# A two-layer hybrid block on one core: triangular inverse and retention issued earlier, six feed-forward columns for one half with their down products under the norm

## The chip, the cores and the metric

One core of a Trainium2 chip runs the whole program. The metric is the device time in microseconds (us), the median of several runs. The engines are TensorE (PE, with its weight loads shown as PEld), VectorE (DVE), ScalarE (ACT), GpSimd (POOL) and SyncE (SP), whose queue issues nearly all transfers. Each engine works through its own instructions in program order; they wait for each other through semaphores.

## What is computed

Two layers over x of 1024 tokens by 1024 columns, float32, each with a mixer of four parts and a feed-forward part:

```python
def hybrid_layer(x, ...):
    p = rms_norm(x, g_pre_mix) @ w_in            # 1024 -> 2824 columns
    y_a = pool_mixer(a_pool, ...)                # windowed means
    y_b = retention_mixer(r_q, r_k, r_v, r_g, cos, sin)   # chunks of 128, 4 heads
    y_c = spatial_gating_mixer(s_u, s_v, ...)
    y_d = deltanet_mixer(d_qkv, d_z, d_b, d_a, ...)       # chunks of 64: triangular solve, then a scan
    x = x + rms_norm(concat(y_a, y_b, y_c, y_d) @ w_out, g_post_mix)
    h = rms_norm(x, g_pre_ffn)
    a, b = split(h @ w_up)                       # 2 x 2816 columns
    a = causal_dwconv(a, conv_w) + conv_b
    return x + rms_norm((gelu(a) * b) @ w_down, g_post_ffn)
```

## The kernel before

The tokens are taken in two halves of 512 (`HALF`), each as four blocks of 128 (`NB`). Every large matrix product is made of three products: weights and activations are split in a high part, cast by ACT (`whi`, L202; L207 for activations), and a low part, the rest, by DVE (`wlo`, L203; L208). `unit()` loads, casts and splits one piece of weights.

For layer l and half h, `win(l, h)` computes the input products and the four mixers, and `out(l, h)` the output product and both norms. In the second layer the feed-forward part is done differently from the first: up products by a scheme of sums and differences of token rows (`build` makes seven combinations A11, S1, S2, A12, S3, Q4, A22; `up_f` makes for one column block f of 128 columns the products of both halves, or of the second half only), with gated results in a DRAM array `gD`, and then a down phase over all 22 blocks f, whose sums stand in eight tiles `acc`. For the first few f, the first half's up product is instead made in the plain way (`plain_up`, L1029 on), before `build`: eight of them, five ahead of `out(1, 1)` and three behind it. These are the work that covers the two norms.

What sets the order: the program is written as a sequence of steps, and a scheduler places every instruction in its engine's queue by its own estimate of the times, with the order of the code as priority; `high_priority(offset)` moves instructions forward. In `win` a string gives the order of ten steps: for `win(1, 1)` it is `ORD1`, with z, s, p, n for input units, g and q for two mixers, u for the retention's units, r for the retention and b for `dn_back`. Ahead of them stands `dn_front`, which makes the triangular matrices `LT`, `AT` and sends their diagonal 32x32 blocks through DRAM to the tile `A`, 64 blocks on 64 partitions. `dn_back` then has three parts: 31 steps on DVE that invert the diagonal blocks in place,

```python
for i in range(1, 32):
    V.scalar_tensor_tensor(pr[:, 0:i, 0:i], A[:, 0:i, 0:i], -1.0, ...)      # L833
    V.tensor_reduce(A[:, 0:i, i], pr[:, 0:i, 0:i], AX.X, ALU.add)           # L835
```

two passes of the inverse through DRAM (d2 to `XT`, and d3 to the small tiles x, which `dn_solve` loads), and four `dn_solve` and four `dn_scan`, one for each block of 128 tokens, whose instructions take turns. `dn_solve` is the chain L876, L884, L893, L899, L908/L910 on PE with DVE and ACT between; `dn_scan` (L938, L953, L956) ends with a head norm on ACT and DVE and a transpose on PE (L962), whose result times `zf` is the last quarter of y. `out(1, 1)` needs all of y.

The last stage, `end_block`, multiplies each block's sum by the norm's weights (`gx`, L1213), half of it on POOL and half on DVE, and adds x.

Of the kernel before, what the change touches and what calls it, by code (L numbers as in the profile page):

```python
# [19 lines left out]
P = 128  # L20
# [15 lines left out]
ORD1 = "zspgqunbr"  # L36
# [21 lines left out]
NPRE, NHALF = 5, 8  # L58
# [60 lines left out]
class Net:  # L119
# [30 lines left out]
    def down_phase(self):  # L150
        self.phase(("pa", 8), ("pr", 2), ("py", 2), ("pw", 6), ("pg", 6))
# [268 lines left out]
    def win(self, l, h, hT, pre=None):  # L420
# [107 lines left out]

        def do_back():
            self.dn_back(l, qf, R["zf"], sc, dn, FAST and (l, h) in QUICK)  # L530
# [4 lines left out]
        steps = dict(n=do_rg, f=do_first, z=do_z, s=do_su, p=do_pool, g=do_sgu, q=do_pmix, u=do_runits, r=do_ret, b=do_back)  # L535
# [287 lines left out]
    def dn_back(self, l, qf, zf, sc, dn, fast):  # L823
        nc, pp, tmp, st, pm = self.nc, self.pp, self.tmp, self.state[l], self.pm[l]
        V = nc.vector
        LT, AT, R0, kt, A2, Dv = (dn[k] for k in ("LT", "AT", "R0", "kt", "A", "Dv"))
# [20 lines left out]
        X = dict(d3=d3, LT=LT, AT=AT, R0=R0, kt=kt, Dv=Dv, XT=XT, qf=qf, zf=zf, sc=sc, MC={})  # L847
# [190 lines left out]


# [6 lines left out]
    def rows(self, l):  # L1046
        names = ("A22", "A12", "Q4", "S3", "S2", "S1", "A11")
        self.A = {}
        for n in names[::-1]:
# [42 lines left out]
    def up_f(self, l, f, halves):  # L1092
# [18 lines left out]
        with self.tc.high_priority(offset=2000):  # L1111
# [52 lines left out]
    def down_full(self, l):  # L1164
# [4 lines left out]
        groups = [[0, 1]] + [list(range(f, f + 4)) for f in range(2, NF, 4)]  # L1169
        for fs in groups:  # L1170
            us, gs = [], []
            for f in fs:
                us.append(self.unit(t["wD"][l, f]))
                r = self.r4("graw")
                nc.sync.dma_start(r, self.gD[l][f])
                g = self.pg.tile([P, 2, SEQ], F32R, tag="g", name="g")
                with self.tc.high_priority(offset=2000):
                    self.split(g[:, 0], g[:, 1], r)
                gs.append(g)
            last = fs is groups[-1]  # L1180
            for b in range(2 * NB):
                tb = slice(b * P, b * P + P)
                for n in range(2):
                    s = slice(n * 512, n * 512 + 512)
                    ps = self.ps() if n else self.pq()
                    for i in range(len(fs)):
                        g, u = gs[i], us[i]
                        nc.tensor.matmul(ps, g[:, 0, tb], u[0][:, s], start=i == 0, stop=False)
                        nc.tensor.matmul(ps, g[:, 0, tb], u[1][:, s], start=False, stop=False)
                        nc.tensor.matmul(ps, g[:, 1, tb], u[0][:, s], start=False, stop=i == len(fs) - 1)  # L1190
# [9 lines left out]
    def end_block(self, l, b, acc, gpost):  # L1200
# [3 lines left out]
        xb = self.py.tile([P, D], F32, tag="xb", name="xb", bufs=6)  # L1204
# [4 lines left out]
        g = self.py.tile([P, D], F32, tag="gx", name="gx")  # L1209
        for n in range(2):  # L1210
            s = slice(n * 512, n * 512 + 512)
            nc.scalar.activation(sq[:, s], acc[:, s], AF.Square, accum_out=ss[:, n:n + 1])
            (nc.gpsimd if n == 0 else V).tensor_tensor(g[:, s], acc[:, s], gpost[:, s], ALU.mult)  # L1213
# [84 lines left out]
    def run(self):  # L1298
# [6 lines left out]
        for l in range(DEPTH - 1):  # L1305
# [8 lines left out]
            y = self.win(l + 1, 1, hT)  # L1314
# [8 lines left out]
        for f in range(2):  # L1323
            self.up_f(l, f, (1,))
        self.build(l, 0)
        half = list(range(2, NHALF))
        for f in range(NHALF, NF):
# [83 lines left out]
```

## Time and profile before

| | us |
|---|---|
| median of 3 runs | 2557.73 (2556.59 to 2560.81) |
| profiled execution | 2557.02, span 2555.2 |
| PE busy | 2431.4 (95% of the span) |
| DVE busy | 1773.3 (69%) |
| ACT busy | 968.4 (38%) |
| POOL busy | 267.0 (10%) |
| mean granted PE clock | 0.974 of full |

The span is what the profile shows; 1.8 us of the profiled execution lie around it. Stages of interest, by their place in the span: `win(1, 1)` from about 1500 to 1800 us, with the bare solve and scan from 1660 to 1728; `out(1, 1)` to about 1853; three plain f to 1888; `build` from 1896 to about 1945; the up phase to 2283; the down phase from 2296 to 2544; the end to 2555. In rows with a bracket, the bracket gives the engine's idle time before the row and what ended it. The granted clock is given as a share of full speed.

### The profile page before, as it was taken

The page shows a single profiled execution, that of the slowest core. Times are in us where ns is not written, and L with a number is a line of the kernel's source. Part 1 is how long each engine was busy: PE and PEld are TensorE (multiplying, and loading weights), DVE is VectorE, ACT ScalarE, POOL GpSimd, SP SyncE. Part 2 cuts the span into 40 slices and gives each one's busy share as a digit, 9 for nine tenths or more (in the row PEclk, how much of TensorE's full clock was granted, in tenths as well). Part 3 has the DMA queues.
Part 4 walks back from the last instruction along what each step waited for, and adds up shares of the span by engine and source line. Part 5 has one row for each costly group of instructions (what it writes and reads, how often), then busy time and mean ns, then how long its engine had stood idle before and what let it go on. Part 6 is the DMA issues. An engine that isn't in the chain of part 4 may idle for free. (4 is left out here: it accounts for less than half of the span.)

```text
span 2555.2 us, 36529 instructions
## 1 busy us (share of the span) xinstructions
PE 2431.4 (95%) x14116; PEld 2031.3 (79%) x14116; DVE 1773.3 (69%) x3657; ACT 968.4 (38%) x1509; POOL 267.0 (10%) x359
## 2 busy tenths in 40 slices
PE   8989998999999999999999999959978999979998
PEld 7968987877788987787788897847967888868886
DVE  8895799765655898855665688956577776653537
ACT  6333452423332553332332355212445444432212
POOL 2221113000000013100000003220011000000001
PEclk9999998999999999999999999968989999999999
DMA  5233442322223552322223354212553222233312
GB/s 182 76 90 102 137 148 72 97 76 83 84 86 124 166 166 69 99 80 79 75 91 97 128 181 165 81 35 72 169 189 112 91 100 87 83 119 128 132 66 83
DMA packets 98482, 274.54 MB, mean 107 GB/s; under 512 B 30258, under 2 KB 30578, under 8 KB 97796
## 3 DMA queue, kind: packets, MB, share of 16 engines
q1 hardware_dynamic: 94532, 259.55, 31.3%
q0 software_dynamic: 3776, 12.65, 1.5%
q8 instruction: 111, 1.82, 0.3%
q14 instruction: 63, 0.52, 0.1%
HBM read 234.39 MB, written 37.78 MB: 107 GB/s over the span
## 5 line engine op out<-in xcount | busy, mean ns | idle before, releaser
L202 ACT CAST whi<-raw 128x1024 fp32r<-128x1024 f32 (+1 forms) x298 | 310.6, 1049 | 679.8 <-PE psg L213 205.4
L212 PE MATMUL psg<-hT,whi 128*128 128x512 f32 x1280 | 510.6, 399 | 2.9 <-ACT whi L202 1.3
L213 PE MATMUL psg<-hT,whi 128*128 128x512 f32 x1280 | 509.0, 398 | 0.2 <-DVE hT L371 0.2
L214 PE MATMUL psg<-hT,wlo 128*128 128x512 f32 x1280 | 508.8, 399 | 0.0
L203 DVE TENSOR_TENSOR wlo<-raw,whi 128x1024 fp32r<-128x1024 f32 (+1 forms) x275 | 338.8, 1237 | 169.5 <-ACT whi L202 165.1
L212 PEld LDWEIGHTS psg<-hT,whi 128*128 128x128 f32 x1280 | 242.1, 189 | 57.5 <-ACT whi L202 1.9
L213 PEld LDWEIGHTS psg<-hT,whi 128*128 128x128 f32 x1280 | 241.8, 189 | 56.0 <-issue 0.6
L214 PEld LDWEIGHTS psg<-hT,wlo 128*128 128x128 f32 x1280 | 241.8, 189 | 55.8 <-issue 0.2
L1245 DVE TENSOR_TENSOR acc<-acc,psg 128x512 f32<-128x512 f32 x160 | 109.0, 686 | 74.7 <-PE psg L1240 74.1
L234 PE MATMUL psg<-wlo,hT 128*128 128x256 f32 (+1 forms) x512 | 148.5, 291 | 5.7 <-DVE wlo L203 5.7
L233 PE MATMUL psg<-whi,hT 128*128 128x256 f32 (+1 forms) x512 | 145.8, 288 | 2.2 <-DVE rqk L512 1.9
L235 PE MATMUL psg<-whi,hT 128*128 128x256 f32 (+1 forms) x512 | 147.3, 289 | 0.0
L233 PE MATMUL psg<-whi,y 128*128 128x256 f32 x512 | 142.5, 283 | 2.4 <-ACT raw L1007 0.9
L1104 ACT CAST w<-wraw 128x512 fp32r<-128x512 f32 x154 | 92.1, 620 | 137.5 <-PE psg L1090 67.4
L234 PE MATMUL psg<-wlo,y 128*128 128x256 f32 x512 | 143.2, 282 | 0.0
L235 PE MATMUL psg<-whi,y 128*128 128x256 f32 x512 | 142.9, 282 | 0.0
L1238 PE MATMUL psg<-whi,g 128*128 128x512 f32 x352 | 141.5, 404 | 0.0
L1105 DVE TENSOR_TENSOR w<-wraw,w 128x512 fp32r<-128x512 f32 x154 | 104.6, 698 | 49.9 <-ACT w L1104 49.4
L1239 PE MATMUL psg<-wlo,g 128*128 128x512 f32 x352 | 138.8, 394 | 0.0
L1240 PE MATMUL psg<-whi,g 128*128 128x512 f32 x352 | 138.6, 394 | 0.0
L833 DVE SCALAR_TENSOR_TENSOR pr<-A 64x1 f32<-64x1 f32 (+30 forms) x124 | 113.2, 913 | 5.8 <-POOL A L829 3.5
L234 PEld LDWEIGHTS psg<-wlo,hT 128*128 128x128 f32 x512 | 98.1, 192 | 8.9 <-DVE wlo L203 6.7
(471 smaller groups left out, 5092.4 us busy)
## 6 DMA issues: line engine op xcount, KB each, us to landing
raw<-in_wU SPq DMA_DIRECT2D x104, 512.0 KB, 3.5
raw<-in_wD SPq DMA_DIRECT2D x66, 512.0 KB, 3.8
raw<-in_wA SPq DMA_DIRECT2D x56, 512.0 KB, 3.6
wraw<-in_wU SPq DMA_DIRECT2D x22, 1024.0 KB, 4.9
raw<-in_wO SPq DMA_DIRECT2D x40, 512.0 KB, 3.8
raw<-in_wB SPq DMA_DIRECT2D x24, 512.0 KB, 3.6
xs<-xb SPq DMA_DIRECT2D x24, 512.0 KB, 3.8
graw<-gD SPq DMA_DIRECT2D x22, 512.0 KB, 4.8
```

What stands on the lines that cost most here:

```text
L202: nc.scalar.copy(hi[:, :n], raw[:, :n])
L203: eng.tensor_tensor(lo[:, :n], raw[:, :n], hi[:, :n].bitcast(F32), ALU.subtract)
L212: nc.tensor.matmul(ps, a[0], b[0], start=first, stop=False)
L213: nc.tensor.matmul(ps, a[0], b[1], start=False, stop=False)
L214: nc.tensor.matmul(ps, a[1], b[0], start=False, stop=last)
L233: self.nc.tensor.matmul(ps[:, :width], h0, hi[:, s], start=k == 0, stop=False)
L234: self.nc.tensor.matmul(ps[:, :width], h0, lo[:, s], start=False, stop=False)
L235: self.nc.tensor.matmul(ps[:, :width], h1, hi[:, s], start=False, stop=k == len(hT) - 1)
L833: V.scalar_tensor_tensor(pr[:, 0:i, 0:i], A[:, 0:i, 0:i], -1.0, A[:, 0:i, i].unsqueeze(1).to_broadcast([64, i, i]), ALU.mult, ALU.mult)
L1238: nc.tensor.matmul(ps, hi[:, tb], us[i][0][:, s], start=i == 0, stop=False)
L1239: nc.tensor.matmul(ps, hi[:, tb], us[i][1][:, s], start=False, stop=False)
L1240: nc.tensor.matmul(ps, lo[:, tb], us[i][0][:, s], start=False, stop=i == len(g0) - 1)
```

## The change

1. The 31 steps and what follows up to the small tiles x become a function of their own, `dn_inverse`, and step i. `ORD1` becomes "iunrzspgqxb": the inverse is first, then the retention with its units, then the rest, x and b.
2. Step x is new: the transposed activations of the first half (`to_hT`) and plain f 0 and 1 (`NFILL`). Four more (2 to 5) stand between `win(1, 1)` and `out(1, 1)`.
3. Six plain f instead of eight (`NPRE` = 6). So `up_f` runs for the second half alone for f 0 to 5, and for both for f 6 to 21. The calls for f 0 and 1 lose their priority of 2000.
4. Behind `out(1, 1)`, in place of three plain f, the new `plain_down`: down products of f 0 to 5 for the first half, 144 products of 512 columns, whose sums go to DRAM (`accD`).
5. The down phase loads `accD` into `acc[0]` to `acc[3]` and makes f 0 to 5 for the second half only, in groups of two and four. The split weights now lie in one tile with the split g (`g`, 4 x SEQ, six buffers); raw weights have two buffers (a pool `pw` of 2), raw g two.
6. `rows` allocates the seven combinations in the order of their use. `end_block` does both halves of gx on DVE; xb has 8 buffers, gx 4.

```diff
-ORD1 = "zspgqunbr"
+ORD1 = "iunrzspgqxb"
-NPRE, NHALF = 5, 8
+NPRE, NFILL = 6, 2
...
-        self.phase(("pa", 8), ("pr", 2), ("py", 2), ("pw", 6), ("pg", 6))
+        self.phase(("pa", 8), ("py", 2), ("pw", 2), ("pr", 2), ("pg", 6))
...
+        def do_inverse():
+            self.dn_inverse(dn)
+
         def do_back():
+            if "XT" not in dn:
+                self.dn_inverse(dn)
             self.dn_back(l, qf, R["zf"], sc, dn, FAST and (l, h) in QUICK)
...
+    def plain_down(self, l):
+        nc, V = self.nc, self.nc.vector
+        self.accD = self.pd.tile([HALF, D], F32, name="accD")
+        us, gs = [], []
+        for f in range(NPRE):
+            raw = self.pw.tile([P, WS], F32, tag="raw", name="raw", bufs=2)
+            nc.sync.dma_start(raw[:, :D], self.t["wD"][l, f])
+            if f < 3:
+                hi = self.pw.tile([P, WS], F32R, tag="hi", name="whi")[:, :D]
+                lo = self.pw.tile([P, WS], F32R, tag="lo", name="wlo")[:, :D]
+            else:
+                w = self.pp.tile([P, 2, D], F32R, tag="big", name="wbig", bufs=4)
+                hi, lo = w[:, 0], w[:, 1]
+            self.split(hi, lo, raw[:, :D])
...
+        for b in range(NB):
...
+                nc.scalar.copy(acc[:, s], ps)
+            nc.sync.dma_start(self.accD[tb], acc)
...
         acc = [self.pa.tile([P, D], F32, tag="acc", name=f"acc{b}") for b in range(2 * NB)]
-        groups = [[0, 1]] + [list(range(f, f + 4)) for f in range(2, NF, 4)]
+        for b in range(NB):
+            nc.sync.dma_start(acc[b], self.accD[b * P:b * P + P])
+        groups = [list(range(0, 2)), list(range(2, NPRE))] + [list(range(f, f + 4)) for f in range(NPRE, NF, 4)]
...
-            for b in range(2 * NB):
+            for b in range(NB if fs[0] < NPRE else 0, 2 * NB):
...
-            (nc.gpsimd if n == 0 else V).tensor_tensor(g[:, s], acc[:, s], gpost[:, s], ALU.mult)
+            V.tensor_tensor(g[:, s], acc[:, s], gpost[:, s], ALU.mult)
...
-        hT = self.to_hT(acc, True)
-        self.plain_up(l, 0, range(NPRE), hT)
+        self.plain_up(l, 0, range(NFILL, NPRE), keep["hT"])
         self.out(l, 1, y, True)
-        self.plain_up(l, 0, range(NPRE, NHALF), hT)
+        self.plain_down(l)
```

How the queues change at three places (a row: line, operation, output from inputs, shape, times in a row; some lines of `dn_solve` and `dn_scan` are 9 further on in the changed kernel, those of the retention 6).

PE before, in `win(1, 1)`, at the first solve: L367 are transposes of the next half's activations, L876 reads the small tiles x (x_99, x_100).

```order
L214 MATMUL psg<-hT_13388,wlo 128x512
L367 MATMUL psg<-ident,acc_13475 128x128
L367 MATMUL psg<-ident,acc_13476 128x128 x4
L367 MATMUL psg<-ident,acc_13477 128x128 x4
L876 MATMUL psm<-x_99,LT 32x32 x8
L876 MATMUL psm<-x_100,LT 32x32 x8
L884 MATMUL psm<-XT,x_99 32x32 x8
L884 MATMUL psm<-XT,x_100 32x32 x8
L893 MATMUL psm<-R_14590,XT 128x128 x8
L899 MATMUL psm<-AT,R_14590 64x128 x4
```

PE now, at the same place (L885 is the former L876):

```order
L586 MATMUL psm<-tmp,pm_7910 128x512
L885 MATMUL psm<-x_99,LT 32x32 x8
L885 MATMUL psm<-x_100,LT 32x32 x8
L214 MATMUL psg<-hT_15706,wlo 128x512
L212 MATMUL psg<-hT_15706,whi 128x512
L213 MATMUL psg<-hT_15708,whi 128x512
L214 MATMUL psg<-hT_15706,wlo 128x512
```

Between the steps of the solve there now stand 23, 20, 21, 6, 7, 3, 9, 2, 9, 19, 13 and 4 products of 512 columns of plain f 2 to 5 (136), and the retention's products are all ahead of it. Behind them come 36 products of `out` and the last two blocks of the scan without anything between, then 18 more of `out`, the last transpose (now L971) and the other 330.

DVE before, within the 31 steps (L203 is the low part of weights):

```order
L833 SCALAR_TENSOR_TENSOR pr<-A 64x27x27
L203 TENSOR_TENSOR wlo<-raw,whi 128x1024
L835 TENSOR_REDUCE A<-pr 64x27
L833 SCALAR_TENSOR_TENSOR pr<-A 64x28x28
L835 TENSOR_REDUCE A<-pr 64x28
L203 TENSOR_TENSOR wlo<-raw,whi 128x1024
```

DVE now, at the same steps: L280 to L286 are single links of the reciprocal root in the retention's head norm, and L625 applies it; the transpose L688 on PE waits for L625's `tmp`.

```order
L682 SCALAR_TENSOR_TENSOR ret_7938<-ret_7938,ck 128x128 x2
L841 TENSOR_REDUCE A<-pr 64x27
L285 SCALAR_TENSOR_TENSOR rt<-rt 128x4
L839 SCALAR_TENSOR_TENSOR pr<-A 64x28x28
L286 SCALAR_TENSOR_TENSOR rs<-rt,rs 128x4
L841 TENSOR_REDUCE A<-pr 64x28
L625 TENSOR_TENSOR tmp<-psm,rs 128x256
L618 TENSOR_REDUCE hs<-tmp 128x4
L839 SCALAR_TENSOR_TENSOR pr<-A 64x29x29
```

The head norm of the retention's first block of tokens is spread over steps 23 to 28, one link to a step or so, and that of the second block over steps 28 to 31 and the rows behind them.

SP before, from the up phase to the down phase (gD is the last up result, graw the loads of it, raw the weights):

```order
L1175 DMA graw<-gD_109 128x1024 x2
L1162 DMA gD_109<-c 128x1024
L1175 DMA graw<-gD_109 128x1024 x2
L200 DMA raw<-in_wD 128x1024 x2
L1175 DMA graw<-gD_109 128x1024 x2
```

SP now:

```order
L1211 DMA acc_20791<-accD 128x1024
L1219 DMA graw<-gD_109 128x1024 x2
L1203 DMA gD_109<-c 128x1024
L1219 DMA graw<-gD_109 128x1024
L1217 DMA wraw<-in_wD 128x1024 x3
```

One load of g instead of two stands ahead of the first weights, and four loads of `accD` ahead of both.

More of the change, by code (lines that the diff above doesn't have):

```diff
@@ L533, in do_first @@
             self.hT1 = self.first_norm(1)
[L535 removed]
+        steps = dict(n=do_rg, f=do_first, z=do_z, s=do_su, p=do_pool, g=do_sgu, q=do_pmix, u=do_runits, r=do_ret, b=do_back,
+                     i=do_inverse, x=mid)
         for k in (ORD0 if (l, h) == (0, 0) else ORD1 if (l, h) in QUICK else ORD):
@@ L821, in dn_front, with dn_inverse @@
         return dict(LT=LT, AT=AT, R0=R0, kt=kt, A=A, Dv=Dv)
-    def dn_back(self, l, qf, zf, sc, dn, fast):
-        nc, pp, tmp, st, pm = self.nc, self.pp, self.tmp, self.state[l], self.pm[l]
+    def dn_inverse(self, dn):
+        nc, pp = self.nc, self.pp
         V = nc.vector
-        LT, AT, R0, kt, A2, Dv = (dn[k] for k in ("LT", "AT", "R0", "kt", "A", "Dv"))
+        A2 = dn["A"]
         A = A2[0:64]
@@ L1037, in plain_up @@
             self.nc.sync.dma_start(self.gD[l][f, :, h * HALF:h * HALF + HALF], c)
+    def plain_down(self, l):
[12 more added lines that the diff above has]
+            self.split(hi, lo, raw[:, :D])
+            us.append((hi, lo))
+            r = self.pa.tile([P, HALF], F32, tag="acc", name="graw")
+            nc.sync.dma_start(r, self.gD[l][f, :, 0:HALF])
+            g = self.r4("g", F32R)
+            self.split(g[:, :HALF], g[:, HALF:], r)
+            gs.append((g[:, :HALF], g[:, HALF:]))
+        for b in range(NB):
+            tb = slice(b * P, b * P + P)
+            acc = self.pa.tile([P, D], F32, tag="acc", name="acc")
+            for n in range(2):
+                s = slice(n * 512, n * 512 + 512)
+                ps = self.ps()
+                for i in range(NPRE):
+                    nc.tensor.matmul(ps, gs[i][0][:, tb], us[i][0][:, s], start=i == 0, stop=False)
+                    nc.tensor.matmul(ps, gs[i][0][:, tb], us[i][1][:, s], start=False, stop=False)
+                    nc.tensor.matmul(ps, gs[i][1][:, tb], us[i][0][:, s], start=False, stop=i == NPRE - 1)
+                nc.scalar.copy(acc[:, s], ps)
+            nc.sync.dma_start(self.accD[tb], acc)
     def cbuf(self, name):
@@ L1046, in rows @@
     def rows(self, l):
-        names = ("A22", "A12", "Q4", "S3", "S2", "S1", "A11")
         self.A = {}
-        for n in names[::-1]:
+        for n in ("A11", "S1", "S2", "A12", "S3", "Q4", "A22"):
             hi = self.pA.tile([P, 4, 512], F32R, tag=f"{n}h", name=f"{n}h")
@@ L1090, in product, with up_f @@
             nc.tensor.matmul(ps, b[:, 1, s], ah[:, k, cs], start=False, stop=k == 3, skip_group_check=sk)
-    def up_f(self, l, f, halves):
+    def up_f(self, l, f, halves, ahead=2000):
         nc, pf = self.nc, self.pf[l]
@@ L1109, in add @@
             V.tensor_tensor(raw[:, o], raw[:, o], raw[:, a], ALU.add)
-        with self.tc.high_priority(offset=2000):
+        with self.tc.high_priority(offset=ahead):
             w11 = cast(2)
@@ L1313, in run, with fill @@
             acc = self.out(l + 1, 0, y)
-            y = self.win(l + 1, 1, hT)
+            keep = {}
+            def fill(a=acc):
+                keep["hT"] = self.to_hT(a, True)
+                self.plain_up(l + 1, 0, range(NFILL), keep["hT"])
+            y = self.win(l + 1, 1, hT, mid=fill)
         l = DEPTH - 1
-        hT = self.to_hT(acc, True)
-        self.plain_up(l, 0, range(NPRE), hT)
+        self.plain_up(l, 0, range(NFILL, NPRE), keep["hT"])
         self.out(l, 1, y, True)
-        self.plain_up(l, 0, range(NPRE, NHALF), hT)
+        self.plain_down(l)
         self.up_phase()
@@ L1322, in run @@
         self.build(l, 1)
-        for f in range(2):
-            self.up_f(l, f, (1,))
+        self.up_f(l, 0, (1,), 0)
+        self.up_f(l, 1, (1,), 0)
         self.build(l, 0)
-        half = list(range(2, NHALF))
-        for f in range(NHALF, NF):
+        half = list(range(2, NPRE))
+        for f in range(NPRE, NF):
             if half:
```

27 lines of the change are left out of this document (16 added, 11 removed).

## The prediction

> **What bounds it now.** First the page: PE is busy nearly all the time, so a gain is either work taken off PE or time in which PE waits or runs slowly.
>
> ```profile
> span 2555.2 us, 36529 instructions
> PE 2431.4 (95%) x14116; PEld 2031.3 (79%) x14116; DVE 1773.3 (69%) x3657; ACT 968.4 (38%) x1509; POOL 267.0 (10%) x359
> ```
>
> Second, the view of busy time by stretches, cut in the second layer where PE waits; the columns are stretch, its length, busy time of PE, PEld, DVE, ACT and POOL, clock, share of the DMA engines, GB/s.
>
> ```profile
> 1600.00:1660.00 60.00, 55.46 (x407) 49.99 (x406) 55.47 (x89) 14.95 (x19) 11.29 (x8) 1.00 0.28 81
> 1660.00:1676.00 16.00, 1.14 (x22) 0.80 (x21) 7.67 (x6) 2.04 (x2) 1.80 (x1) 0.61 0.47 112
> 1676.00:1692.00 16.00, 15.51 (x296) 13.61 (x296) 8.90 (x28) 6.13 (x20) 2.60 (x10) 0.86 0.03 6
> 1692.00:1708.00 16.00, 10.80 (x111) 7.65 (x108) 8.64 (x34) 1.95 (x6) 4.17 (x13) 0.78 0.11 35
> 1708.00:1728.00 20.00, 10.68 (x56) 8.31 (x56) 14.29 (x40) 5.75 (x12) 7.00 (x10) 0.50 0.02 7
> 1728.00:1742.00 14.00, 11.64 (x36) 8.48 (x37) 8.58 (x14) 1.96 (x4) 1.98 (x3) 0.50 0.10 39
> 1760.00:1888.00 128.00, 126.04 (x758) 110.03 (x756) 80.99 (x178) 53.86 (x86) 0.00 (x0) 1.00 0.49 165
> 1888.00:1945.00 57.00, 37.73 (x262) 34.60 (x260) 45.24 (x73) 28.57 (x53) 15.65 (x14) 0.79 0.45 155
> 2340.00:2380.00 40.00, 40.00 (x174) 32.36 (x173) 19.06 (x23) 8.11 (x8) 0.00 (x0) 1.00 0.29 100
> ```
>
> Length less busy time is idle; busy time times (1 - clock) is lost to the clock. From 1600 to 1742 that is 4.5 + 14.9 + 0.5 + 5.2 + 9.3 + 2.4 = 36.8 us idle and 0.4 + 2.2 + 2.4 + 5.3 + 5.8 = 16.1 us by the clock: 52.9 us, the largest sum the change can touch. Third, the waits of PE from 1655 to 1745, and the rows that end them.
>
> ```profile
> PE psm L876 <- DMA x<-d: 14.7, 1, 14.7
> PE psh L962 <- DVE tmp L619: 12.4, 3, 5.5
> 1675.20 1.42 PE L876 MATMUL psm<-x,LT 128*32 128x32 f32 x32 [14.72 <-DMA x<-d]
> 1701.39 0.69 PE L962 MATMUL psh<-ident,tmp 128*128 128x128 f32 x2 [3.44 <-DVE tmp L619]
> 1722.11 0.66 PE L962 MATMUL psh<-ident,tmp 128*128 128x128 f32 x2 [5.50 <-DVE tmp L619]
> ```
>
> The solve waits for the inverse, whose 31 steps fill DVE from 1612.7 on, 10.7 us after PE ended the last product ahead of it (first row), and for other work among them:
>
> ```profile
> 1601.58 0.38 PE L806 MATMUL psm<-qf,kf 64*128 64x128 f32 x2
> 1612.74 0.90 DVE L833 SCALAR_TENSOR_TENSOR pr<-A 64x1 f32<-64x1 f32 x1
> 1613.85 1.14 DVE L833 SCALAR_TENSOR_TENSOR pr<-A 64x4 f32<-64x4 f32 x1
> 1615.21 0.16 DVE L833 SCALAR_TENSOR_TENSOR pr<-A 64x9 f32<-64x9 f32 x1
> 1666.62 1.15 DVE L835 TENSOR_REDUCE A<-pr 64x31 f32<-64x961 f32 x1
> L203 DVE TENSOR_TENSOR wlo<-raw,whi 128x1024 fp32r<-128x1024 f32 x7 | 8.5, 1211 | 1.8 <-ACT whi L202 1.8
> L512 DVE TENSOR_TENSOR rqk<-psg,ck 128x256 f32<-128x256 f32 x8 | 3.3, 408 | 0.0
> L371 DVE TENSOR_TENSOR hT<-psh,hT 128x512 fp32r<-128x512 f32 x4 | 2.7, 680 | 0.1
> L279 DVE TENSOR_SCALAR rs<-rs 128x4 int32<-128x4 int32 x4 | 0.7, 167 | 0.1
> ```
>
> **The solve (step order, inverse first, fill).** The code ahead of the inverse's loads is as much PE work as before (144 products of 512 columns and 244 of 256, against 277 of 512), so it ends near 1600. The pitch of 512-column products is (1883.35 - 1879.61)/16 = 0.234 us; 256 columns take half, 0.117.
>
> ```profile
> 1879.61 0.40 PE L214 MATMUL psg<-hT,wlo 128*128 128x512 f32 x1
> 1883.35 0.39 PE L212 MATMUL psg<-hT,whi 128*128 128x512 f32 x1
> ```
>
> The order puts 344 products of 512 columns (80 us), 44 of 256 (5 us) and the small products of retention, transposes and mixers (some 24 us, an estimate) ahead of the first solve, so PE arrives at about 1709, without any wait. The inverse ended at 1667.8 and x was there 7.4 us later, at 1675.2; a few us later now makes 1680. That wait of 14.7 us goes. Then 136 products (32 us) stand between the steps of solve and scan that were bare.
>
> What is late next? First, the retention, which is now under the inverse. PE gets to its first transpose (L688) after 44 x 0.117 + 165 x 0.234 + 4.5 for small products = 48 us, at 1648, and the second is 9 us of work behind it, 1657. Both wait for a head norm whose links stand one by one among the steps. Before, the loop took 1667.8 - 1612.7 = 55.0 us with 11.9 us of other work in it (seven L512 of 0.41, six L203 of 1.21, two L577 of 0.91). Now the order has among the steps five low parts (6.1), ten operations of 256 columns (taken as L512, 4.1), four of half that (0.8), an L371 (0.7) and 15 links (L279, 2.5): 14.2 us, so 57 to 58. Its data come 10.7 us after the front, as before, so it runs from 1611 to 1669, and the last link of the second norm is 3 us behind that, with a low part in it: 1672. PE loses 1672 - 1657 = 15 us in two waits. A wait of 5.5 us was followed by 20 us at clock 0.50, but with sparse work; behind these waits there are dense products, and I take 2 us each, 4 in all.
>
> Second, the tail of the scan. The last two blocks are still bare: waits of 3.4 and, with 18 products (2.1 us) ahead of the last transpose, 5.5 - 2.1 = 3.4. Behind it, `out` needs the cast and low part of the last quarter of y (row below: 2.35 us for two), some 2.5. Half clock over some 7 busy us costs 3.
>
> ```profile
> 1725.48 2.35 DVE L208 TENSOR_TENSOR y<-zf,y 128x512 fp32r<-128x512 f32 x2
> ```
>
> With 1 us elsewhere, 15 + 4 + 6.8 + 2.5 + 3 + 1 = 32 us stay lost of 52.9: **-21 us**. Bounds: with no wait in the retention 13 stay (-40); with the bare tail at half clock up to the end of the transition, 42 (-11).
>
> **Two plain f fewer.** A plain f with its half costs 48 x 0.234 + 84 products of 256 columns at 0.113 (three pitches in the rows below), 20.7 us; the full one 84 x 0.234 = 19.7. Two: **-2 us**. The down products number 1056 either way (144 + 912).
>
> ```profile
> 2005.32 0.28 PE L1089 MATMUL psg<-A11l,w 128*128 128x256 f32 x1
> 2005.66 0.28 PE L1089 MATMUL psg<-A11l,w 128*128 128x256 f32 x1
> ```
>
> **`plain_down` under the norms.** Three plain f were 144 products, and so is it: 33.7 us of cover as before. Its weights of f 3 to 5 use slots that the last quarters of y hold until `out` ends; 27 products (6.3 us) come first, against one load (3.8 us, the median of the page), a cast and a low part (1.05 by the row below, and L203's 1.21): **+1**, from 0 to +4.
>
> ```profile
> L202 ACT CAST whi<-raw 128x1024 fp32r<-128x1024 f32 (+1 forms) x298 | 310.6, 1049 | 679.8 <-PE psg L213 205.4
> raw<-in_wD SPq DMA_DIRECT2D x66, 512.0 KB, 3.8
> ```
>
> Six splits of weights and six of g lie on DVE and ACT, busy 81 and 54 of 128 us there. The load of hn stood behind a store of gD and now behind one of accD:
>
> ```profile
> 1889.19 0.34 SPq L1037 DMA_DIRECT2D gD<-c  x1
> 1889.70 1.09 SPq L1063 DMA_DIRECT2D hn<-hnD  x2
> 1895.92 1.09 PE L1076 MATMUL psg<-ident,hn 128*128 128x128 f32 x4 [7.55 <-DVE w L1105]
> ```
>
> So the wait at `build` stays: 0, within 2 of it. The lost priority of `up_f` 0 and 1 hardly moves a row: 0.
>
> **Down layout.** Before the first down product, the last raw of g held the weights back on SP:
>
> ```profile
> 2288.20 1.46 SPq L1175 DMA_DIRECT2D graw<-gD  x2
> 2289.70 0.90 SPq L200 DMA_DIRECT2D raw<-in_wD  x2
> 2295.93 0.80 PE L1188 MATMUL psm<-whi,g 128*128 128x512 f32 x1 [13.16 <-ACT whi L202]
> ```
>
> With one such load ahead instead of two the weights go 0.7 to 1.5 us sooner: **-1**. The four loads of `accD` (2 MB) are issued while the up phase ends. The first group is 48 products now, 11 us, and f 2 to 5 must come through two buffers each: loads of two tiles (6 us from issue to PE above), two casts and two low parts (4.5 us) for each f, against 4.2 us of PE for each. The queue lets f 2 be ready about when it is needed: 0, up to +6.
>
> **gx on DVE.** Eight operations of 512 columns move from POOL, 1.29 us each, to DVE, where the L371 above takes 0.68; the last block's chain behind the last product runs on DVE already: 0, within 1.
>
> ```profile
> L1213 POOL TENSOR_TENSOR gx<-acc,gpost x8: 1263/1290/1738, 2509.6 to 2543.7; 128x512 f32<-128x512 f32 x8
> ```
>
> **Sum:** -21 - 2 + 1 - 1 = -23, on the profiled execution's 2557.0: 2534 us. That execution is 0.7 below the median, less than I can tell apart.
>
> **Rivals.**
> 1. The retention doesn't wait under the inverse, because PE comes later than I count or the steps run faster (two of the first steps took 0.90 and 1.14 us where the next took 0.16). Then 15 + 4 stay off: 2515. For it: DVE and PE drift together in the order; against: the norm's last links stand behind step 31.
> 2. The clock stays down. From 1708 to 1742 it was 0.50 through 22 us of busy time between waits. If 20 more busy us run at 0.50, the 9 between the retention's two waits and some 11 from the first bare block into `out`, another 10 us go: 2544. The Trainium skill, page "TensorE: Matmul & The Clock Gate", section "Part 1: The HAM clock gate", says that an idle window of about 3.4 us halves the clock and a busy one of that length restores it. By that rule each of four waits costs 1.7 us, 7 in all, where I take 7; the trace agrees in 1660 to 1676, where 14.9 idle us left 0.61. The section "HAM oscillation — how this bites in real kernels" of that page of the Trainium skill speaks for this rival: bursts shorter than the waits between them each start cold.
> 3. Slower. The down phase starves: with two buffers for raw weights and g, each group's third and fourth f are loaded only as the first two are split. The price is 6 + 2.3 = 8 us for a group, five groups: 40, so 2574; it decides from 23/5 = 4.6 us a group. Against: in the row from 2340 the DMA engines are busy for 0.29 and DVE for 19 of 40 us, and one group is 45 us of PE.
> 4. No change: PE still comes to the solve before x, because weights for plain f 2 to 5 are late behind the inverse on DVE. The 14.7 us stay, with the waits of the retention: about 2553. Against: 29 us lie between 1680 and 1709.
>
> **Chances.** Forecast (2525 to 2542) 0.50, rival 1 0.22, rival 2 0.17, rival 3 0.05, rival 4 0.06. Range 2511 to 2551: from rival 1 with -4 for its bounds, to rival 2 with the +4 and +3 of `plain_down` and the down phase. 0.2% is 5 us, about what a measurement can tell from no change: faster (below 2552.6) 0.50 + 0.22 + 0.17 and some of rival 4, 0.90; same 0.05; slower 0.05.
>
> **What would show it.** A wait on L885 for x gone; waits on L688 for L625's tmp of 15 us in sum between 1648 and 1672; two waits of about 3.4 us on L971; a wait of 7 us on the transposes of `build` and of 12 on the first down product. The forecast is wrong if L688 doesn't wait, if L885 does, or if rows of the down phase after its first product show PE idle by more than 6 us.

## Result and the profile after the change

| | before | after |
|---|---|---|
| median, us | 2558.15 (2556.59 to 2560.81, 4 runs) | 2527.69 (2523.48 to 2531.13, 4 runs) |
| ratio, 95% interval | | 0.988 (0.986 to 0.990) |
| profiled execution, us | 2557.02, span 2555.2 | 2523.48, span 2521.5 |

30.5 us off, where 23 were forecast. The profiled execution of after lies 4.2 us below its median. Call the last product of `dn_front` in `win(1, 1)` the front product. Up to it, the program is nearly the same in before, after and nine of the kernels below, and yet this product starts anywhere between 1598.2 and 1606.6 us in their profiles; so stages are compared by their lengths below, not by their places.

The page of after:

```profile
span 2521.5 us, 36340 instructions
PE 2420.2 (96%) x14020; PEld 2019.6 (80%) x14020; DVE 1772.1 (70%) x3659; ACT 972.2 (39%) x1510; POOL 253.3 (10%) x351
```

PE is busy 11.2 us less than before (96 matmuls fewer) in a span that is 33.7 us shorter. The rest is time in which PE no longer waits. Busy time by stretches, with the columns of the prediction's table:

```profile
1600.00:1660.00 60.00, 56.19 (x274) 45.98 (x273) 53.79 (x106) 18.61 (x26) 6.05 (x3) 0.94 0.25 79
1660.00:1676.00 16.00, 12.79 (x76) 9.94 (x75) 12.48 (x24) 7.95 (x12) 1.80 (x1) 1.00 0.51 119
1676.00:1692.00 16.00, 16.00 (x88) 13.60 (x88) 11.78 (x37) 4.14 (x7) 2.13 (x2) 1.00 0.15 50
...
1742.00:1760.00 18.00, 18.00 (x177) 14.00 (x171) 12.92 (x32) 7.49 (x17) 2.37 (x7) 1.00 0.45 141
1760.00:1780.00 20.00, 16.86 (x150) 13.37 (x148) 13.02 (x35) 7.13 (x14) 3.24 (x10) 0.87 0.35 112
1780.00:1800.00 20.00, 14.88 (x98) 12.84 (x99) 10.17 (x34) 5.46 (x10) 1.22 (x3) 0.70 0.08 26
1800.00:1836.00 36.00, 34.97 (x287) 34.05 (x286) 23.00 (x49) 18.07 (x29) 0.00 (x0) 1.00 0.67 214
...
2340.00:2380.00 40.00, 40.00 (x178) 33.10 (x178) 17.47 (x22) 5.36 (x6) 0.00 (x0) 1.00 0.32 105
```

From 1600 to 1800 us, 3.8 + 3.2 + 3.1 + 5.1 = 15 us are idle and 3.4 + 2.2 + 4.5 = 10 us go to the clock: 25 us, where 52.9 were lost up to 1742 before and 32 were forecast. The stretches from 1676 to 1760, where the solve now is, have no idle time at all. The last row has 178 matmuls in 40 us, where before had 174: that is new, and the prediction has nothing on it.

PE's waits from 1600 to 1810 us (total, times, longest):

```profile
PE psh L971 <- DVE tmp L625: 4.8, 2, 3.4
PE psm L688 <- DVE tmp L625: 2.8, 1, 2.8
PE psg L233 <- ACT y L207: 2.2, 2, 1.2
```

The rows of PE's timeline that have to do with retention's last transposes, L688 (the bracket is the wait):

```profile
1652.85 0.66 PE L688 MATMUL psm<-ident,tmp 128*128 128x128 f32 x2 [2.83 <-DVE tmp L625]
1663.74 0.66 PE L367 MATMUL psh<-ident,acc 128*128 128x128 f32 x4 [0.54 <-DVE hT L371]
1665.47 0.66 PE L367 MATMUL psh<-ident,acc 128*128 128x128 f32 x4 [1.07 <-DVE hT L371]
1667.43 0.66 PE L367 MATMUL psg<-ident,acc 128*128 128x128 f32 x4 [1.31 <-ACT ap L434]
1667.92 0.38 PE L688 MATMUL psm<-ident,tmp 128*128 128x128 f32 x2
```

There is no wait on L885: x is there long before PE. L688 waits once, and its second transpose runs without a wait, at the time at which the prediction would have it wait until 1672.

SP's queue at the end of the up phase, as rows of the timeline:

```profile
2273.71 14.48 SPq L1211 DMA_DIRECT2D acc<-accD  x4
2288.29 1.13 SPq L1219 DMA_DIRECT2D graw<-gD  x2
2298.02 0.32 SPq L1219 DMA_DIRECT2D graw<-gD  x1
2298.39 6.81 SPq L1217 DMA_DIRECT2D wraw<-in_wD  x3
```

The wait of the first down product, from the view of waits:

```profile
PE psm L1234 <- ACT g L207: 16.7, 1, 16.7
```

The four loads of `accD` stand in front of the others and wait 14.5 us for the memory of the `acc` tiles, which the up phase still holds. The first weights are loaded 10 us behind them, since the third load of raw g, which stands between, goes out only at 2298.0. PE waits 16.7 us instead of 13.2.

By lengths of stages, from the first and last products of each in the trace (us):

| | before | after | work moved | gain (-) or loss | forecast |
|---|---|---|---|---|---|
| front product to end of `out` | 251.4 | 238.3 | +13.8 (a plain f more, 11.2; and 2.6 that stood ahead of the front product before) | -26.9 | -21 |
| to the first transpose of `build` | 42.8 | 46.0 | 0 | +3.2 | +1 |
| to the last up product | 386.9 | 404.4 | +20.4 (f 6 and 7 for both halves) | -2.8 | 0 |
| to the first down product | 13.2 | 16.7 | 0 | +3.6 | -1 |
| down phase | 247.9 | 208.8 | -33.4 (144 products) | -5.7 | 0 |
| to the end | 11.3 | 9.0 | 0 | -2.3 | 0 |

The 2.6 us are the difference of 144 products of 512 columns and 244 of 256 from 277 of 512 (at 0.234 and 0.117 us), which stand ahead of the front product. The work moved sums to +0.8 us in the rows, to -1.8 with these (forecast -2), the gains and losses to -30.9. This execution came 3.5 us sooner to the front product, 2.6 of them by less work. Together, but for rounding, that is the 33.7 of the spans.

The table compares one execution with one. Five kernels below (the first of experiment 5, the three of experiment 7 and that of experiment 8) have the same program up to the up phase. Their first stage has 239.1 to 241.1 us, their second 47.8 to 48.6: a gain of 24 to 26 us instead of 26.9, and a loss of 5.0 to 5.8 instead of 3.2.

### The profile page after: what moved, and what is told of

The parts are those of the page before. It is cut to its first block, busy times and chain, and to the rows that moved or that the text cites. A ratio compares the mean times of both kernels' runs of the same rounds, so it can differ in the third digit from the quotient of the medians.

```text
span 2521.5 us, 36340 instructions
## 1 busy us (share of the span) xinstructions
PE 2420.2 (96%) x14020; PEld 2019.6 (80%) x14020; DVE 1772.1 (70%) x3659; ACT 972.2 (39%) x1510; POOL 253.3 (10%) x351
## 4 chain that ended last, share of the span: by engine, by line
PE 77%; DVE 14%; issue 3%; DMA 3%; ACT 2%; POOL 0%; SPq 0%; DVEq 0%; POOLq 0%; ACTq 0%
PE psg L213 9%; PE psg L214 9%; PE psg L212 9%; PE psg L1284 3%; PE psg L1286 3%; PE psg L1285 3%; PE psg L233 3%; PE psg L234 3%; DVE pr L839 3%; PE psg L235 3%; PE psg L1129 3%; PE psg L1131 3%; PE psg L1130 3%; DVE wlo L203 2%; DVE A L841 2%
## 5 line engine op out<-in xcount | busy, mean ns | idle before, releaser
L213 PE MATMUL psg<-hT,whi 128*128 128x512 f32 x1248 | 497.3, 398 | 0.4 <-DVE hT L371 0.4
L212 PE MATMUL psg<-hT,whi 128*128 128x512 f32 x1248 | 497.3, 399 | 0.1
L214 PE MATMUL psg<-hT,wlo 128*128 128x512 f32 x1248 | 495.6, 398 | 0.0
L202 ACT CAST whi<-raw 128x1024 fp32r<-128x1024 f32 (+1 forms) x272 | 283.4, 1049 | 534.0 <-PE psg L213 209.8
L203 DVE TENSOR_TENSOR wlo<-raw,whi 128x1024 fp32r<-128x1024 f32 (+1 forms) x249 | 307.5, 1240 | 143.8 <-ACT whi L202 139.7
L213 PEld LDWEIGHTS psg<-hT,whi 128*128 128x128 f32 x1248 | 235.7, 189 | 54.9 <-issue 0.9
L214 PEld LDWEIGHTS psg<-hT,wlo 128*128 128x128 f32 x1248 | 235.6, 189 | 54.3 <-issue 0.4
L212 PEld LDWEIGHTS psg<-hT,whi 128*128 128x128 f32 x1248 | 235.6, 189 | 53.0 <-issue 0.4
```

What stands on the lines that cost most here:

```text
L202: nc.scalar.copy(hi[:, :n], raw[:, :n])
L203: eng.tensor_tensor(lo[:, :n], raw[:, :n], hi[:, :n].bitcast(F32), ALU.subtract)
L212: nc.tensor.matmul(ps, a[0], b[0], start=first, stop=False)
L213: nc.tensor.matmul(ps, a[0], b[1], start=False, stop=False)
L214: nc.tensor.matmul(ps, a[1], b[0], start=False, stop=last)
```

## Experiments

Each kernel was timed beside the kernel before, whose median in these batches was 2557.1 to 2559.8 us. A ratio and its interval are against that; a difference of medians from different batches is uncertain by some us.

**1. The order alone, on the kernel before.** Five plain f ahead of `out`, two of them as step x, eight in all, the old down layout:

```diff
-ORD1 = "zspgqunbr"
+ORD1 = "iunrzspgqxb"
-NPRE, NHALF = 5, 8
+NPRE, NHALF, NFILL = 5, 8, 2
```

> The kernel before with the new step order of win(1,1) alone: inverse and retention first, two of the five plain f as the step x, still eight plain f, the old down layout and gx half on POOL. Theory (the gain is the bare solve and scan): the 52.9 us lost between 1600 and 1742 fall to about 25, as in the changed kernel, so -27 +-4 us: about 2531. Rival (the gain comes from the down phase and the work placed under the norm): less than -15 us, above 2543.

Measured: 2541.25 us, ratio 0.992 (0.991 to 0.994), 0.0076 x 2558 = 19 us: more than the rival's 15, but less than the 27 +-4 that I expected. From the front product to the end of `out` 232.2 us, 19.2 less than before with 2.6 us more work, so some 22. The order thus makes two thirds of the gain. Of what is left, 2 to 5 us lie in this same stage (L971 waits 6.9 us here, 4.8 in after); the rest is behind it.

**2. The two plain f as a cover, with the old order of the rest.** In the changed kernel, the inverse is issued with the solve again and retention stands last:

```diff
-ORD1 = "iunrzspgqxb"
+ORD1 = "zspgqunxbr"
```

> The changed kernel with the steps of the last window in the order of before and only the two plain f added ahead of the solve (ORD1 = zspgqunxbr): the inverse is issued just before the solve again, and retention after it. Theory 'retention's place is the gain': its transposes and norms come last, with nothing beside them, and 15 to 25 us of the 27 us gained between the last front product and out come back: 2543 to 2553. Rival 'the two plain f that stand ahead of the solve are the gain, whatever stands last': 2528 to 2535.

Measured: 2558.52 us, ratio 0.9997 (0.9989 to 1.0006), 31 us above the changed kernel: more than I expected, all of what the change as a whole gained. The stage from the front product to the end of `out` is 270.8 us, 32.5 longer than in the changed kernel. Four of PE's waits there, in the timeline:

```profile
1784.05 0.66 PE L971 MATMUL psh<-ident,tmp 128*128 128x128 f32 x2 [5.48 <-DVE tmp L625]
1793.57 1.23 PE L659 MATMUL psm<-tmp 64*128 64x128 f32 x8 [3.77 <-ACT tmp L653]
1807.27 0.66 PE L688 MATMUL psm<-ident,tmp 128*128 128x128 f32 x2 [3.83 <-DVE tmp L625]
1825.27 0.66 PE L688 MATMUL psm<-ident,tmp 128*128 128x128 f32 x2 [3.66 <-DVE tmp L625]
```

Busy time by stretches (columns: stretch, length, busy time of PE, clock, DMA share, GB/s):

```profile
1680.00:1760.00 80.00, 80.00 (x643) 1.00 0.35 102
1760.00:1800.00 40.00, 24.94 (x151) 0.66 0.23 81
1800.00:1840.00 40.00, 30.05 (x177) 0.66 0.08 27
```

The solve is covered here too (1680 to 1760 has no gap). But two blocks of retention come last, with nothing beside them: 80 us hold 25.0 us of idle time, and the 55 busy ones run at 0.66, which costs another 18.7. A cover for one chain is no gain if the chain that it had been covering becomes bare.

**3. Retention ahead of the fill, the inverse where it was.**

```diff
-ORD1 = "iunrzspgqxb"
+ORD1 = "zspgqunrxb"
```

> As e9_fill_only, but with retention's step put ahead of the two plain f (ORD1 = zspgqunrxb) and the inverse still issued with the solve, so that retention stands between the inverse and the fill and not behind the scan. e9 stood at 2558.5, the changed kernel at 2527.7. Theory 'retention's place alone is the gain': 2526 to 2534, and no waits on L651, L659 or L688 behind 1760 us. Rival 'the inverse has to be issued first too': 2543 or more, with a wait on the solve's L885 or a later end of the inverse.

Measured: 2535.24 us, ratio 0.992 (0.990 to 0.993): 23 of the 31 us come back, between the two theories. The waits on L651, L659 and L688 behind 1760 us are gone, as the first theory has it; the inverse ends 16 us later (1680.8 against 1664.7), which costs the solve nothing, but the last blocks of the scan wait longer (L971: 10.4 us in two, against 4.8). So retention's place is the larger part. What is left, 7.5 us by medians, goes with issuing the string's first steps in the new order. The stage is 245.7 us, 7.4 longer than in after, with 2.6 us less work in it; that this and the medians give nearly the same number is in part chance, since the first down product waits 12.1 us here and 16.7 in after (experiment 7).

**4. The new down layout without `plain_down`.** The kernel of experiment 1, with the weights split into the tile of their g:

```diff
-        self.phase(("pa", 8), ("pr", 2), ("py", 2), ("pw", 6), ("pg", 6))
+        self.phase(("pa", 8), ("py", 2), ("pw", 2), ("pr", 2), ("pg", 6))
...
-                us.append(self.unit(t["wD"][l, f]))
+                raw = self.pw.tile([P, D], F32, tag="raw", name="wraw")
...
+                g = self.pg.tile([P, 4, SEQ], F32R, tag="g", name="g")
```

> The kernel before with the new order of steps (as in e1_order, 8 plain f, no plain_down), and now also the new layout of the down phase: weights split into the tile of their g, two buffers of raw weights. Theory 'the pitch comes with the layout': the down phase falls from 246.8 us to 1056 products x 0.227 + 7 = 241.5 us, so 5 us below e1: 2536 (2533 to 2539). Theory 'the pitch comes with the missing tail of the mix phase or with plain_down': as e1, 2541. What is then left to the changed kernel's 2527.7 is plain_down with its two fewer plain f, and the norm scale on DVE, 8 us (of which the norm scale is 2.5 by e3_gx_pool).

Measured: 2530.47 us, ratio 0.989 (0.988 to 0.991); the down phase 242.0 us instead of 246.8, as expected (4.8 against 5.3). The medians are 11 us apart, more than this; by the ratios it is 7 with some 5 either way, which holds it. So 1056 products of the same shape take 0.0046 us less each, with no product taken away. `plain_down`, the two plain f and gx together are then worth little, net of the longer wait on the first down product (16.7 us in after, 11.8 here): this kernel is within 3 us of the changed one.

**5. Is it that operands lie in one tile, or where they start?** First, in the changed kernel, the split g moved 256 bytes against the weights inside the tile:

```diff
-                g = self.pg.tile([P, 4, SEQ], F32R, tag="g", name="g")
+                gf = self.pg.tile([P, 4 * SEQ + 128], F32R, tag="g", name="g")
+                o = lambda i, k: gf[:, i * SEQ + k:i * SEQ + k + SEQ]
+                w0, w1, g0, g1 = o(0, 0), o(1, 0), o(2, 64), o(3, 64)
```

> The changed kernel with the split g moved by 256 bytes against the split weights in the same tile (and xb with 7 buffers for the room). In the changed kernel every product of the down phase starts 0.227 us after the one before, where all other stages and the down phase before take 0.231 to 0.234. Theory A (the pitch depends on where the two operands start modulo 512 bytes): 0.230 to 0.235 again, 912 x 0.005 = 4 to 5 us slower. Theory B (it depends on both lying in one tile, or on the traffic beside): 0.227 stays, no change.

Measured: 2529.69 us, ratio 0.989 (0.987 to 0.991), pitch 0.227 us as before the shift. That excluded a dependence on 512 bytes, and left smaller steps, the tile and the traffic. So the products were measured by themselves, in 28 sequences that differ only in byte addresses:

> Only x is copied into the output; the rest is 28 sequences of matmuls on one region of SBUF, with no DMA and no other engine beside them. 17 have the shape of the down products (128x128 stationary, 128x512 moving, 192 each), 6 that of the input products, 5 that of the output products with 256 columns; they differ only in the byte addresses of the operands. In the full kernel the 128x512 products have a pitch of 0.227 us in the new down phase and 0.232 elsewhere. Theory 'alignment': a sequence where both operands start at the same offset modulo 256 bytes shows 0.227, one with stationary and moving 64 or 128 bytes apart, or with tiles of 4224 bytes, shows 0.232. Theory 'distance': the sequences with both operands in one 16 KB piece show 0.227, those with the operands in separate regions 0.232, whatever the alignment. Theory 'traffic': the addresses have nothing to do with it, it is what other engines and DMAs write and read in SBUF meanwhile; all 17 sequences of the down shape agree within 0.001 us.

Busy time of PE in 40 us taken from inside a sequence (columns as in experiment 2; the count in brackets is what matters). In this order: both operands 64 bytes past a multiple of 256; the stationary one 64 bytes further on than the moving one; 128; 256; tiles of 4224 bytes as in `unit()`; separate aligned regions; only the low parts 64 off; stationary 64 off in a separate region:

```profile
53.00:93.00 40.00, 40.00 (x179) 1.00 0.00 1
183.00:223.00 40.00, 40.00 (x173) 1.00 0.00 0
230.00:270.00 40.00, 40.00 (x174) 1.00 0.00 0
273.00:313.00 40.00, 40.00 (x178) 1.00 0.00 0
317.00:357.00 40.00, 40.00 (x174) 1.00 0.00 1
405.00:445.00 40.00, 40.00 (x178) 1.00 0.00 1
492.00:532.00 40.00, 40.00 (x175) 1.00 0.00 1
537.00:577.00 40.00, 40.00 (x173) 1.00 0.00 0
...
1020.00:1060.00 40.00, 40.00 (x343) 1.00 0.01 1
1111.00:1151.00 40.00, 40.00 (x335) 1.00 0.00 1
```

The ten sequences of the down shape whose operands start at the same offset modulo 256 bytes all have a pitch of 0.2267 to 0.2270 us, in one piece or in separate regions; the seven others have 0.2290 to 0.2333, by the size and sign of the difference. No other engine was busy in these stretches. So "alignment" holds, and "distance" and "traffic" fall. All offsets tried are multiples of 64 bytes. The input form shows the same (0.2267 aligned; 0.2313 with the kernel's addresses). The last two rows are the form of 256 columns, first with the kernel's own unaligned addresses, then with aligned ones, and here it is the other way round: 0.1175 us against 0.1200.

**6. Aligned operands everywhere.** The changed kernel with other addresses only:

```diff
+WT = 1088
-            hi = self.pw.tile([P, WS], F32R, tag="hi", name="whi")
-            lo = self.pw.tile([P, WS], F32R, tag="lo", name="wlo")
+            hi = self.pw.tile([P, WT], F32R, tag="hi", name="whi")[:, o:]
+            lo = self.pw.tile([P, WT], F32R, tag="lo", name="wlo")[:, o:]
-            us = [self.unit(ap, 4 * width) for ap in aps]
+            us = [self.unit(ap, 4 * width, o=16) for ap in aps]
...
+    def pad(self, n):
+        self.nc.gpsimd.memset(self.pz.tile([P, n], F32, name="pad"), 0.0)
```

> The changed kernel with the addresses of operands alone changed: weight tiles of the mixing and the first FFN layers 4352 bytes instead of 4224, 192 bytes of pad ahead of the transposed inputs and 64 ahead of the up phase's matrices, so that stationary and moving operand of every 128x512 product start at the same offset modulo 256; the weights of the 256-column products are put 64 bytes into their tiles, since that form was faster apart (0.1178 against 0.1200 in the study of addresses). Theory 'alignment sets the pitch, and TensorE is the bound nearly everywhere': 3744 input products x 0.0055, 1056 down products of the first layers' FFN x 0.006, some 1740 up products x 0.0055 give 36 us; with what waits take back, 25 to 36 us: 2492 to 2503. Rival 'ACT, DVE and the clock gate set the pace of the windows, and a faster product only waits longer': the up phase alone gains, 9 us: 2518.

Measured: 2507.29 us, ratio 0.980 (0.978 to 0.981), 20 us below the changed kernel: between the theories, nearer the first. The matmuls in 200 us of the up phase, after and here (columns as above):

```profile
2000.00:2200.00 200.00, 200.00 (x914) 1.00 0.24 87
```

```profile
2000.00:2200.00 200.00, 200.00 (x928) 1.00 0.24 86
```

The median pitch is 0.227 in every group of 128x512 products, the input products (0.232 to 0.233 in after), the first layers' FFN (0.230 to 0.236) and the up products among them. The up phase gains 6.6 us where 9 were counted: it has 1344 products of 512 columns and not 1740, and its 504 of 256 columns now start aligned too, with a median pitch of 0.120 us where after has 0.113, some 3 us more. The front product comes at 1586.1, 16 us ahead of the mean of six kernels (1602, after and the five with its program up to there), where 3744 input products and the first layers' FFN should give up to 27. PE's busy time ahead of it is 1542.7 us against 1560.0 to 1565.1 in the six, its idle time 43 against 38 to 43. So waits took back only a few us of the 27, against the rival; PE's busy time itself fell by some 19 us and not by 27, and why is not shown.

**7. The wait on the first down product.** First the loads of `accD` issued only ahead of the products of f 6 to 9:

```diff
-        for b in range(NB):
-            nc.sync.dma_start(acc[b], self.accD[b * P:b * P + P])
...
+            if fs[0] == NPRE:
+                for b in range(NB):
+                    nc.sync.dma_start(acc[b], self.accD[b * P:b * P + P])
```

> The changed kernel with the four loads of accD issued ahead of the loads of f 6 to 9 instead of ahead of all loads of the down phase. Theory (the wait of 16.7 us before the first down product comes from these loads, which wait 14.5 us for tiles on SP and hold the loads of g and the weights behind them): the wait falls to 11 to 12 us and the time by 4 to 6 us. Rival (the weights wait for SBUF of the up phase anyway): the wait stays at 16 to 17 us, no change.

Measured: 2526.52 us, ratio 0.987 (0.986 to 0.989), which can't be told from the changed kernel by time; in the trace the wait falls from 16.7 to 12.0 us. So these loads cost the 4.7 us by which the forecast of this step was off, and 12 us have another cause. It is not their place in the queue as such. In the kernels of experiments 2 and 3 they stand first too, but the last up products come in another order there, and the loads wait only 9.2 us for their tiles (the row is of experiment 2); the first down product then waits 12.0 and 12.1.

```profile
2315.00 9.24 SPq L1211 DMA_DIRECT2D acc<-accD  x4
```

By the kernel's layout, the buffer of the first raw weights shared its first 192 bytes with the last buffer for p1 of the up phase. A pad of 256 bytes takes them apart:

```diff
+        pad = self.pz.tile([P, 64], F32, name="pad")
```

> The changed kernel with the four accD loads issued only ahead of the products of f 6 to 9 (as in e2_accd_late), and a pad of 256 bytes ahead of the raw weights of the down phase, so that their first buffer no longer shares its first 192 bytes with a buffer of the up phase that is written until the last f. The first weights can then be loaded once A11's last product is done, about 25 us before the up phase ends, and their loads stand ahead of the last store of g on SP's queue. Theory 'the wait on the first down product is the wait of its weights for memory': 12.0 us (e2) falls to 0 to 4 us, the time to 2517 to 2521. Rival 'the split on ACT and DVE, or the store of the last g, ends last anyway': the wait stays above 9 us, the time 2524 to 2528.

Measured: 2526.52 us, ratio 0.988 (0.986 to 0.989). The wait falls to 4.7 us, near the 0 to 4 expected, but the time doesn't move: the down phase grew from 208.9 to 216.2 us. The wait of down products (total, times, longest), in the view of waits:

```profile
PE psm L1237 <- ACT g L207: 8.9, 2, 4.7
```

The stretches behind the first wait:

```profile
2300.00:2320.00 20.00, 19.37 (x85) 1.00 1.02 402
2320.00:2340.00 20.00, 15.78 (x63) 0.91 0.79 283
```

The second wait, of 4.2 us, comes at the 103rd of the 912 products, in the second group and not in the third, as my expectation below has it. It ends with the split of the raw g of f 5, whose load was issued at 2311.0 and is there at 2325.3:

```profile
2325.30 1.04 ACT L207 CAST g<-graw 128x1024 fp32r<-128x1024 f32 x1 [7.44 <-DMA graw<-gD]
```

Before it, the DMA engines are busy all the time (1.02 of the stretch, 402 GB/s). Six of the eight loads of xb, 3 MB that nobody needs before the last group, are issued between 2298.7 and 2301.8. With all eight put behind the last weights, into two tiles g that have come free (the pad grows by xb's old room, so that the other buffers stay where they are):

```diff
-        nc.gpsimd.dma_start(xb, self.xs[2 * l][rows])
+                xts = [self.pg.tile([P, 4, SEQ], F32, tag="g", name="xb") for _ in range(2)]
+                xbs = [xts[b // 4][:, b % 4] for b in range(2 * NB)]
+                for b in range(2 * NB):
+                    nc.sync.dma_start(xbs[b], self.xs[2 * l][b * P:b * P + P])
```

> e8_pad, with the eight loads of xb (512 KB each, for the last addition) issued behind the last weights into two tiles of the down products that have come free, so that they no longer run beside the first weights of the down phase (there DMA stood at 1.02 of the span between 2300 and 2320 us, and the third group waited). Theory 'these loads took the bandwidth': the down phase falls from e8's 216 us to 209, the first wait stays below 5 us, the time is 2526.5 - 7 = 2519 (2516 to 2522). Rival 'SP's queue and the two buffers of raw weights set the pace of the loads': the down phase stays at 213 or above, 2524 or more.

Measured: 2520.32 us, ratio 0.985 (0.983 to 0.986), as the first theory has it. The wait stays at 4.7 us, the down phase is 209.7 us, and the same stretches read:

```profile
2300.00:2320.00 20.00, 19.87 (x78) 0.88 0.88 308
2320.00:2340.00 20.00, 19.76 (x88) 1.00 0.81 275
```

**8. gx back on POOL**, its first half only, in the changed kernel:

```diff
-            V.tensor_tensor(g[:, s], acc[:, s], gpost[:, s], ALU.mult)
+            (nc.gpsimd if n == 0 else V).tensor_tensor(g[:, s], acc[:, s], gpost[:, s], ALU.mult)
```

> The changed kernel with half of gx back on POOL. Theory: nothing on the path changes, within 1 us of the changed kernel. Rival: the POOL operations of 1.29 us stretch the small DVE operations beside them in the last blocks, 1 to 3 us slower.

Measured: 2532.64 us, ratio 0.989 (0.988 to 0.991); the intervals of the two overlap, but the stage from the last product to the end is 11.8 us instead of 9.0, near the three other kernels with gx on POOL (11.3, 11.3 and 12.1). Why is seen in the kernel before, at its last product:

```profile
2543.67 1.26 POOL L1213 TENSOR_TENSOR gx<-acc,gpost 128x512 f32<-128x512 f32 x1 [4.45 <-DVE rs L278]
2543.81 1.13 DVE L280 SCALAR_TENSOR_TENSOR rt<-rs 128x1 f32<-128x1 f32 x1
2544.98 0.16 DVE L281 TENSOR_TENSOR rt<-rt,rv 128x1 f32<-128x1 f32 x1
```

A link of one column takes 1.13 us instead of 0.16, and ends when POOL's gx does (2543.67 + 1.26 = 2544.93). This chain of the block before the last stands ahead of the last block's addition on DVE. In after, with no gx on POOL, all 24 links of this kind take 0.15 or 0.16 us. The Trainium skill, page "SBUF — State Buffer", section "🔬 SBUF: two separate sides", has a rule for this: a pair of ports that DVE and GpSimd share goes to one instruction whole, and the other engine waits; it counts for a DVE operation with two inputs in SBUF against one of GpSimd that reads SBUF, as here. The rows agree.

**9. Everything together** (6 and 7):

> e10 and e11 together: the gains add, since they lie in different stages: 2527.7 - 30 - 9 = 2489 (2480 to 2496). Rival 'the faster products only meet the same loads sooner': above 2500.

Measured: 2496.76 us, ratio 0.975 (0.974 to 0.977), 31 us below the changed kernel and 2.5% below the one before. The gains add as expected (20.4 + 7.4 = 27.8 by medians of 6 and 7). The time lies just above the range of 2480 to 2496, by what experiment 6 fell short.

## Why the prediction held, and where its terms were off

The forecast was 2534, with 2525 to 2542 for its own case; 2527.7 is in it. The mechanism of the largest term, the solve and the retention under a cover, is the one described. That the sum came so near is partly luck: the down phase and the end gained 8.0 us by causes that the prediction doesn't have, and the losses ahead of them (`build` and the first down product) were 6.8 us larger than forecast. By terms:

- **The solve's wait for x (-14.7).** Right: no wait is left, and 1676 to 1760 has no idle time.
- **The retention's waits (19 us stay).** The size was wrong: 2.8 us idle in the first wait, 2.9 in three waits of L367 and 3.4 by the clock, some 9. The first wait ends at 1652.9. The second transpose, which I had at 1657 waiting for a norm at 1672, came at 1667.9: PE was held back by transposes of the next half's activations (L367) in between, and the norm's last operation (L625, the last row below) ran from 1667.2 to 1667.6, just ahead of it. Both ends of the term were off, and both to the good: the loop took 54.3 us (1610.49 to 1664.74) where I had 57.5. The same waits, one of 1.8 to 2.9 us on L688 and none at the second, stand in the five kernels with the same program. The condition of rival 1 thus came half true.

```profile
1610.49 0.15 DVE L839 SCALAR_TENSOR_TENSOR pr<-A 64x1 f32<-64x1 f32 x1 [4.05 <-POOL A L835]
1663.61 1.14 DVE L841 TENSOR_REDUCE A<-pr 64x31 f32<-64x961 f32 x1
1667.15 0.42 DVE L625 TENSOR_TENSOR tmp<-psm,rs 128x256 f32<-128x256 f32 x1
```

- **The tail of the scan (12.3 us stay).** 4.8 us in two waits of L971 (1.4 and 3.4, forecast 3.4 each), 2.2 for y, in all 8.2 idle and 6.7 by the clock from 1760 to 1800: 15. Rival 2 did not come: the clock was 0.87 and 0.70 there, and full from 1800 on; in all it cost 10 us where I took 7 and the rival 17. By lost time the whole stage has 52.9 - 25 = 28 us, less 1.0 idle behind 1800; its length gives 26.9. The work ahead of the front product was not as much as before, as I had it, but 2.6 us less; without this the stage would seem to gain 24.4.
- **Two plain f fewer (-2).** The work moved is -1.8. The up phase was 2.8 us shorter than its work beyond that; why is not shown.
- **`plain_down` (+1, 0 to +4).** +3.2 in this execution, in its bounds, but +5.0 to +5.8 in the five others with this program, outside. Nor is it all `plain_down`'s: the kernels of experiments 1 and 4, with three plain f in its place, have 45.7 and 45.4 us here, +2.9 and +2.6 against before. PE does wait for splits of weights and g, as I counted (3.2 us in after, 1.8 of them on the weights of f 3 to 5), and the wait at `build` is 6.2 instead of 7.5.
- **Up to down (-1).** Wrong in sign, +3.6. I counted the four loads of `accD` as traffic, and not as instructions that wait at the head of SP's queue for tiles that the up phase still holds (14.5 us). With them later the wait was 12.0 (experiment 7), 1.1 below before's, as the forecast had it for one load of g fewer.
- **The down phase (0 to +6).** -5.7, by a cause that I did not think of: 912 products at 0.227 instead of 0.232 us, 4.7 us (experiments 4 and 5). The working had a slip too: PE has 24 products, 5.6 us, and not 4.2 for each of f 2 to 5. Rival 3, a down phase that starves, was priced with the loads of the down operands alone; it did show, in the second kernel of experiment 7, once the first wait was gone and xb's loads ran beside the weights.
- **gx on DVE (0, within 1).** -2.3 to -2.8 (experiment 8). The price of the operation was right and beside the point; its neighbour on DVE was what paid.

## What to carry to other kernels

A chain that is bare is not helped by cover alone: ask which chain loses its cover, and put first the one whose length is set by another engine (here 31 steps on DVE), so that the others run under it. Read the pitch of equal products stage by stage; where it differs at full clock, look at the byte offsets of their operands. A load that waits for its tile holds everything behind it on its queue, so see which old buffer each new one lies on, and issue what is needed late behind what is needed soon.

## What the runs showed of the hardware that I had not expected

- The pitch of 128x512 float32r products depends on the start of the stationary against the moving operand modulo 256 bytes: 0.227 us where they agree, 0.229 to 0.233 where they don't. For 256 columns it is 0.120 where they agree and 0.1175 to 0.118 where they don't (0.113 in the up phase of after, 0.120 there once aligned). The Trainium skill, page "TensorE: Matmul & The Clock Gate", section "Step-by-step: what each phase is for", says that the engine reads its two operands through two independent ports and that loading weights takes nothing from the running product. From this alone one would not expect the addresses to matter; the measurement decides. What in the machine makes the difference, the runs don't show.
- The same program came to the same product, some 1600 us into the span, with a spread of 8 us between six kernels (1598.2 to 1606.4). The granted clock up to there is 0.99 in each, and PE's idle time 38 to 43 us. Differences of a few us between spans say nothing without the lengths of the stages, and even these vary: the same stage of some 240 us by up to 2.8.
